# The order of two head pairs in RWKV's and HGRN2's steps, and an issue order between their products

## Chip, core and metric

The kernel runs on one core of one Trainium2 chip, as one program. The metric is the device time of a run in microseconds. One execution was recorded by the hardware profiler; the times of the others are without a profile.

## What is computed

One inference step of a decoder trunk with two layers, for 256 prompt tokens and 8 sequences of 8 new tokens (320 columns in all, width 1024, fp32). A layer is a SwiGLU block, a mixer and a second SwiGLU block. The mixer has three groups of heads beside each other: HGRN2 (4 heads of 64), RWKV-7 (4 heads of 64) and latent attention (8 heads, with a paged cache of 2048 positions for the samples):

```python
for l in range(DEPTH):
    x = x + 0.5 * swiglu(rms_norm(x, W['norm_ffn1'][l]), W['ffn1_wi'][l], W['ffn1_wo'][l])
    p = rms_norm(x, W['norm_mix'][l]) @ W['w_in'][l]
    p_hg, p_rw, p_mla = jnp.split(p, [HG_COLS, HG_COLS + RW_COLS], axis=-1)
    o_hg, hg_s = hgrn2_mixer(p_hg, lbs[l], W['hg_norm'][l], hg_s0[l])
    o_rw, rw_s, rw_sh = rwkv7_mixer(p_rw, rw_sh0[l], rw_s0[l], l, W)
    q_nope, q_pe, c, k_pe = mla_project(p_mla, pos, l, W)
    o_mla = attend(l, q_nope, q_pe, c, k_pe)
    x = x + jnp.concatenate([o_hg, o_rw, o_mla], axis=-1) @ W['w_out'][l]
    x = x + 0.5 * swiglu(rms_norm(x, W['norm_ffn2'][l]), W['ffn2_wi'][l], W['ffn2_wo'][l])
```

RWKV-7 and HGRN2 are recurrences over the tokens. The kernel computes them in blocks of 64 tokens (the samples are a fifth block).

## The kernel before

Activations lie transposed, 128 channels by 320 columns. Dense products take each weight as a rounded part and a remainder in fp32r, three matmuls a tile, and write the PSUM banks `pd`, in the SwiGLU blocks `pr` and `pa` too. Each raw weight block is split by ScalarE (`w<-raw`, L434) and VectorE (L435).

In the mixer several Python generators are woven together by `weave`. In the first part these are the RWKV recurrence (`rw`, then `rw_out`), the rest of the input projection (`rin`, `hg_in`, called `fill`) and the samples' attention (`sample`); in the second part HGRN2 (`hg`), the prompt's attention (`prompt`), the samples' attention still, and the output projection (`w_out`). Each generator gives out a piece of work and says how long its results will take. `weave` keeps a running estimate of TensorE's time, lets the recurrences go as soon as they are due, and fills the time between with the others. A planner then orders each engine's queue when the program is built: it goes by priority (the recurrences and the prompt have a higher one) and by its own estimate of when an instruction's inputs and its PSUM bank are ready. What it has ordered, an engine executes in that order.

Four heads are two pairs of heads (`hp` 0 and 1). A pair's two heads lie in partitions 0 to 63 and 64 to 127, so its small products come in twos on a quarter of the array each (64*64). Each fp32 matmul is two records in the trace. Every pair has a generator of its own, and `together` advances both by one step in each round; a round is a *step* below. The steps of a pair in RWKV are: preparation (elementwise), first products and factors, ten steps of five levels that double an inverse (`X` is evacuated by ScalarE at L1145, the others by VectorE at L1165 and L1171, the factors at L1110), then twelve steps of the recurrence over four blocks of 64 tokens: `R` (L1238), `U` (L1246), and state and output (L1256, L1267), with the samples' block spread over the first of them; at last three steps of `rw_out`. HGRN2 has transposes, exponentials, an elementwise step, and seven steps of products.

Both pairs, in RWKV and in HGRN2, take their PSUM banks from one tag, `pr`, which has three:

```python
    BANKS = {"pd": 2, "pr": 3, "pa": 2, "pv": 1}

    def mm(self, out, w, x, start, stop):
        ...
        self.last = self.nc.tensor.matmul(out, w, x, start=start, stop=stop)
```

A level step and its banks, as an example (L1140 to L1171):

```python
            px = self.bank("pr")
            ...
            nc.scalar.copy(X[:, :n], v5(px, n))
            t0 = self.pe
            if lv < 3:
                factors(1, (0, 1, 2, 3) if lv == 1 else (4,))
```

Of the kernel before, what the change touches and what calls it, by code (L numbers as in the profile page):

```python
# [263 lines left out]
class Kern:  # L264
# [279 lines left out]

    def together(self, *gens):

        gens = list(gens)
        while gens:
            r = None
            for g in list(gens):  # L550
                try:
                    r = next(g)
                except StopIteration:
                    gens.remove(g)
            if gens:
                yield r

# [998 lines left out]
```

## Time and profile before

| | |
|---|---|
| median of 3 runs | 1659.08 us (1657.4 to 1660.34) |
| profiled execution | 1657.07 us |
| its span, first to last instruction | 1655.1 us |
| TensorE busy (matmul) | 1615.0 us, 98% |
| VectorE, ScalarE, GpSimd busy | 957.8, 716.0, 83.6 us |
| mean granted clock of TensorE | 0.993 of full speed |

The span lies 2.0 us below the profiled execution's own time. The mixers lie at about 245 to 606 us (layer 0) and 1064 to 1420 us (layer 1); RWKV's steps at 300 to 457 and 1120 to 1266 us, HGRN2's after them.

### The profile page before, as it was taken

To read this page: it belongs to the slowest core of one execution; us is meant where nothing else is said; L and a number is where in the kernel's file an instruction comes from. 1 tells how busy PE (TensorE), PEld (TensorE's weight loads), DVE (VectorE), ACT (ScalarE), POOL (GpSimd) and SP (SyncE) were. 2 spreads that over 40 slices of the span, in tenths; PEclk is the share of its full clock that TensorE was granted. 3 is DMA by queue.
4 is the path that set the end of the run, shared out by engine and by line. 5 is a ranking of instruction groups with operands and counts; after the bars stand their busy time and mean duration, and the time that the engine had idled before them with its cause. 6 is when DMAs were issued, how large, how long until landed. Compare 5 with 4: busy or idle time off the path is not lost.

```text
span 1655.1 us, 33369 instructions
## 1 busy us (share of the span) xinstructions
PE 1615.0 (98%) x13138; PEld 1441.2 (87%) x13138; DVE 957.8 (58%) x1593; ACT 716.0 (43%) x1207; POOL 83.6 (5%) x118
## 2 busy tenths in 40 slices
PE   8999999999999899999999999999999999999998
PEld 8999998776657599999999999987766676999997
DVE  7555448853445585555465554479444665755543
ACT  6444434543353364444344443346333534544432
POOL 0000000200022000000000000012000310000000
PEclk9999999999999999999999999999999999999999
DMA  8444536646673464445445544365457644454442
GB/s 284 148 149 150 153 90 183 179 134 193 182 219 91 143 215 146 150 153 149 147 149 153 148 147 152 100 187 178 118 173 212 205 134 147 151 149 153 153 146 90
DMA packets 131899, 260.82 MB, mean 158 GB/s; under 512 B 17872, under 2 KB 76816, under 8 KB 131744
## 3 DMA queue, kind: packets, MB, share of 16 engines
q1 hardware_dynamic: 118912, 237.34, 47.5%
q10 hardware_dynamic: 12800, 21.30, 4.3%
q8 instruction: 103, 1.69, 0.4%
q0 software_dynamic: 32, 0.07, 0.1%
q14 instruction: 52, 0.43, 0.1%
HBM read 253.52 MB, written 4.47 MB: 156 GB/s over the span
## 4 chain that ended last, share of the span: by engine, by line
PE 88%; DVE 5%; ACT 3%; DMA 2%; issue 1%; SPq 1%; ACTq 0%; DVEq 0%
PE pd L293 33%; PE pr L293 31%; PE pa L293 18%; PE pv L293 4%; DVE w L435 1%; PE pa L297 1%; ACT S L924 1%; DMA cn<-in_cn 1%; DMA raw<-in_wm 1%; DMA ct<-in_ct 1%; DMA xT<-in_x 0%; DVE kS L458 0%; ACT w L434 0%; DVE rt L1073 0%; ACT L924 0%
## 5 line engine op out<-in xcount | busy, mean ns | idle before, releaser
L435 DVE TENSOR_TENSOR w<-raw,w 128x1024 fp32r<-128x1024 f32 (+1 forms) x390 | 412.6, 1060 | 320.1 <-ACT w L434 313.4
L434 ACT CAST w<-raw 128x1024 fp32r<-128x1024 f32 (+1 forms) x390 | 353.2, 910 | 420.5 <-PE pd L293 192.4
L293 PE MATMUL pd<-xh,w 128*128 128x320 f32 x1792 | 423.7, 316 | 8.3 <-ACT w L434 7.1
L293 PEld LDWEIGHTS pd<-xh,w 128*128 128x128 f32 x1792 | 305.2, 189 | 25.5 <-issue 11.4
L293 PE MATMUL pd<-xl,w 128*128 128x320 f32 x896 | 279.9, 314 | 0.0
L293 PE MATMUL pr<-xh,w 128*128 128x320 f32 x1056 | 240.2, 310 | 0.0
L293 PE MATMUL pa<-xh,w 128*128 128x320 f32 x896 | 201.7, 309 | 0.0
L293 PEld LDWEIGHTS pr<-xh,w 128*128 128x128 f32 x1056 | 178.3, 188 | 0.5
L293 PEld LDWEIGHTS pd<-xl,w 128*128 128x128 f32 x896 | 169.7, 189 | 4.9 <-issue 3.5
L293 PE MATMUL pr<-xl,w 128*128 128x320 f32 x528 | 162.5, 309 | 0.0
L293 PE MATMUL pd<-hh,w 128*128 128x320 f32 x704 | 158.2, 309 | 0.0
L293 PE MATMUL pr<-hh,w 128*128 128x320 f32 x704 | 158.2, 309 | 0.0
L293 PEld LDWEIGHTS pa<-xh,w 128*128 128x128 f32 x896 | 151.0, 188 | 0.0
L293 PE MATMUL pa<-xl,w 128*128 128x320 f32 x448 | 137.6, 309 | 0.0
L293 PE MATMUL pa<-ct,qlat 96*64 96x256 f32 x768 | 122.4, 391 | 2.6 <-ACT qlat L994 1.8
L293 PEld LDWEIGHTS pr<-hh,w 128*128 128x128 f32 x704 | 118.4, 188 | 0.0
L293 PEld LDWEIGHTS pd<-hh,w 128*128 128x128 f32 x704 | 118.4, 188 | 0.0
L293 PE MATMUL pr<-hl,w 128*128 128x320 f32 x352 | 108.8, 309 | 0.0
L293 PE MATMUL pd<-hl,w 128*128 128x320 f32 x352 | 108.8, 309 | 0.0
L482 ACT ACTIVATE fa<-fa 128x320 f32<-128x320 f32 x88 | 41.4, 472 | 134.7 <-DVE fa L481 134.7
L293 PEld LDWEIGHTS pr<-xl,w 128*128 128x128 f32 x528 | 99.1, 188 | 0.3
L293 PEld LDWEIGHTS pa<-ct,qlat 96*64 96x64 f32 x768 | 60.6, 137 | 38.4 <-issue 12.2
(388 smaller groups left out, 1996.6 us busy)
## 6 DMA issues: line engine op xcount, KB each, us to landing
raw<-in_wf SPq DMA_DIRECT2D x264, 512.0 KB, 3.6
ct<-in_ct SPq DMA_DIRECT2D x256, 144.0 KB, 3.0
cn<-in_cn SPq DMA_DIRECT2D x256, 128.0 KB, 2.3
raw<-in_wm ACTq DMA_DIRECT2D x76, 256.0 KB, 3.1
raw<-in_wm SPq DMA_DIRECT2D x50, 256.0 KB, 3.5
xT<-in_x SPq DMA_DIRECT2D x4, 320.0 KB, 6.8
wukt<-in_wukt SPq DMA_DIRECT2D x2, 576.0 KB, 5.5
S<-in_rws SPq DMA_DIRECT2D x4, 256.0 KB, 2.9
```

The costliest lines, as they stand in the source:

```text
L293: self.last = self.nc.tensor.matmul(out, w, x, start=start, stop=stop)
L297: self.nc.tensor.transpose(out, x, ident)
L434: self.cast = nc.scalar.copy(h, src).ins
L435: nc.vector.tensor_tensor(out=lo, in0=src, in1=h.bitcast(F32), op=ALU.subtract)
L482: nc.scalar.activation(a, a, AF.Silu)
L924: nc.scalar.activation(S[p, ch], S[p, ch], AF.Exp, bias=m[:, 5:6], scale=MLA_SCALE, accum_out=m[:, ch:ch + 1])
```

## The change

In each round of `together` the generator that goes second has its TensorE instructions queued behind the last matmul that the first one issued. This is an order of issue, recorded as an edge without a semaphore; instructions of other streams may still stand between. After each round the list is reversed: the pair that went second goes first in the next. Both apply to RWKV (`rw`, `rw_out`) and to HGRN2 (`hg`). Nothing else is changed.

```diff
     def together(self, *gens):
 
+
         gens = list(gens)
         while gens:
-            r = None
+            r, last = None, None
             for g in list(gens):
                 try:
-                    r = next(g)
+                    with self.tc.issue_after(last) if last else ExitStack():
+                        r = next(g)
                 except StopIteration:
                     gens.remove(g)
+                last = self.last.ins
+            gens.reverse()
             if gens:
                 yield r
```

## Rows read from the trace of the kernel before

**Rows 1.** The page: the span and, from part 1, the engines' busy time.

```profile
span 1655.1 us, 33369 instructions
...
PE 1615.0 (98%) x13138; PEld 1441.2 (87%) x13138; DVE 957.8 (58%) x1593; ACT 716.0 (43%) x1207; POOL 83.6 (5%) x118
```

**Rows 2.** Windows, busy us of PE, PEld, DVE, ACT, POOL; clock; DMA share, GB/s.

```profile
300.00:457.00 157.00, 154.71 (x1790) 110.12 (x1789) 87.35 (x169) 66.28 (x138) 15.15 (x21) 0.99 0.59 170
...
1120.00:1266.00 146.00, 140.94 (x1714) 100.79 (x1712) 80.47 (x156) 64.34 (x133) 15.14 (x21) 1.00 0.55 161
```

**Rows 3.** Timeline of TensorE, layer 0's recurrence: start us, us, what, records.

```profile
391.62 0.33 PE L293 MATMUL pr<-R,rwa 64*64 64x64 f32 x4
391.88 1.94 PE L293 MATMUL pa<-ct,qlat 96*64 96x256 f32 x14
393.75 0.66 PE L297 MATMUL pa<-cf,S 128*128 128x128 f32 x4
394.16 0.39 PE L293 MATMUL pd<-xh,w 128*128 128x320 f32 x1
394.48 0.33 PE L293 MATMUL pr<-R,rwa 64*64 64x64 f32 x4
394.74 0.42 PE L293 MATMUL pd<-xl,w 128*128 128x320 f32 x1
```

**Rows 4.** Timeline of TensorE, the same product in a later step.

```profile
433.13 0.45 PE L293 MATMUL pr<-R,rwa 64*64 64x64 f32 x8
433.51 1.51 PE L293 MATMUL pv<-cn,PT 128*64 128x256 f32 x10
```

**Rows 5.** Timeline of TensorE, a short S run and the inside of an F run.

```profile
400.03 0.65 PE L293 MATMUL pv<-cn,PT 128*64 128x256 f32 x4
400.61 0.33 PE L293 MATMUL pr<-Rs,rwa 64*64 64x64 f32 x4
...
441.71 0.46 PE L293 MATMUL pd<-xh,w 128*128 128x320 f32 x2
442.00 0.31 PE L293 MATMUL pd<-xl,w 128*128 128x320 f32 x1
```

**Rows 6.** Timeline: first and last 64*64 run of four stretches (22, 16, 20, 13).

```profile
384.12 1.07 PE L293 MATMUL pr<-S,kkr 64*64 64x512 f32 x4
...
440.91 0.33 PE L293 MATMUL pr<-NK,U 64*64 64x64 f32 x2
...
498.25 0.45 PE L293 MATMUL pr<-hq,hk 64*64 64x64 f32 x8
...
533.05 0.40 PE L293 MATMUL pr<-lf,S 64*64 64x8 f32 x8
...
1198.32 0.33 PE L293 MATMUL pr<-nat,NK 64*64 64x64 f32 x4
...
1251.49 0.33 PE L293 MATMUL pr<-NK,U 64*64 64x64 f32 x2
...
1316.35 0.62 PE L293 MATMUL pr<-hq,hk 64*64 64x64 f32 x14
...
1346.60 0.27 PE L293 MATMUL pr<-AT,EX 64*64 64x64 f32 x1
```

**Rows 7.** Timeline of a wait in layer 0; waits of 1120:1266 (us, times, longest).

```profile
343.25 1.28 ACT L1333 ACT_TABLE_LOAD   x1
...
345.78 0.74 ACT L1145 COPY X<-pr 128x320 f32<-128x320 f32 x2
...
346.25 1.09 PE L293 MATMUL pr<-kkr,bk 64*64 64x128 f32 x16 [2.00 <-ACT X L1145]
...
PE pr L293 <- ACT rwv L1267: 2.1, 1, 2.1
PE pr L293 <- ACT X L1145: 2.0, 1, 2.0
```

**Rows 8.** Groups by line and shape: an evacuation of the recurrence (busy, mean ns).

```profile
L1246 ACT COPY U<-pr 128x64 f32<-128x64 f32 x16 | 3.3, 210 | 22.2 <-PE pr L293 22.2
```

## Prediction

> **What bounds the kernel now.** I read the page first. TensorE is busy 1615.0 of 1655.1 us [rows 1], so I looked at what fills that time rather than at idle time. Next came the windows of the stages that `together` drives. In both layers the RWKV stage keeps TensorE at 154.71 of 157.00 us and 140.94 of 146.00 us, with VectorE and ScalarE near half [rows 2]. The matmul queue sets the length of these stages: time saved in it is time saved, as long as other products are at hand to fill it.
>
> Then I read the timeline of TensorE inside the recurrence, where a pattern shows. Three kinds of product take turns: dense ones on the whole array (128*128, F below), the sample's attention (96*64 and 128*64, S below), and the head pairs' own small ones (64*64 into `pr`, H below). The reader is to see one and the same step of the two pairs at 391.62 and at 394.48 us: R times `rwa`, four records each, with S and F work between them [rows 3]. Forty microseconds on, both pairs' R products stand together as one row of eight at 433.13 [rows 4]. So the planner sometimes joins the pairs and mostly does not.
>
> **What a run costs.** A run here is a stretch of one kind. Start to start, the H run of four takes 391.88 - 391.62 = 0.26 us and the run of eight 433.51 - 433.13 = 0.38 us [rows 3, 4]. Four more records therefore cost 0.12 us, and a run pays 0.26 - 0.12 = 0.14 us for being a run. S: four records take 400.61 - 400.03 = 0.58 us [rows 5], fourteen take 393.75 - 391.88 = 1.87 us [rows 3]. Four records are a pair of products (two sequences side by side), fourteen are three and a half, and a half pair takes as long as a whole one, so (1.87 - 0.58) / 3 = 0.43 us a pair and 0.58 - 0.43 = 0.15 us a run. F: two records take 442.00 - 441.71 = 0.29 us inside a run, 0.145 each; a single one between others takes 394.48 - 394.16 = 0.32 us [rows 3, 5], so about 0.18 us a run. If one H run joins another and its two neighbours of one kind grow together, TensorE saves 0.14 + 0.15 = 0.29 us (S) or 0.14 + 0.18 = 0.32 us (F). I take 0.30 us.
>
> **The change part by part.** Nothing is added to or taken from any engine's work: each matmul, copy and transfer stays, and the number of instructions too. Three things move.
>
> *The tie.* The second pair's matmuls of a step stand behind the last matmul of the first pair's. It orders the queue and is no wait in itself. Without the reversal it would often leave a gap, since the pair that goes second is evacuated second.
>
> *The reversal.* The pair that was last goes first. Its inputs are the last to be ready; the other pair's have then been ready longer, and follow at once. So the joint run starts when the later pair could have started anyway. What is delayed is the pair that was ready earlier. It is off the path: the recurrence of layer 0 runs from 384.12 to 441 us for 12 steps [rows 6], about 4.7 us a step, while an evacuation there takes 210 ns [rows 8]. Work of the other streams covers the delay; if that cover ran out, each step would cost the gap between the pairs, in rows 3 up to 394.48 - 391.62 = 2.9 us, or 24 such steps 69 us. TensorE's busy share in rows 2 speaks against that, and I count nothing.
>
> *Engines and queues behind.* On VectorE and ScalarE the pairs' evacuations swap places in every second step, same work. On SP the loads of the states and the stores of the results swap in the same way between two transfers of equal size; nothing on TensorE waits for the one and not the other. I count nothing for both.
>
> *How many runs join.* In the recurrence I count 22 H runs in layer 0 and 20 in layer 1, for 12 steps each; in HGRN2's products 16 and 13, for 7 steps [rows 6], which hold the first and the last run of each stretch. One run a step would leave 38, so 10 + 8 + 9 + 6 = 33 runs could vanish. The ten steps between (the doubling of the inverse) already have about one run a step, and I expect nothing of them. Not all 33 will join: the pairs share the three `pr` banks. In the recurrence, a step of one pair takes one bank in 5 of 12 steps, two in 5 and three in 2 (read from the code). With one each, both pairs fit; with two or three, the second pair's later product needs a bank that is not yet evacuated, and the planner puts other work before it. The bounds are 0 and 33; I take half, 16, since the steps that fit freely are about that share.
>
> The sum: 16 x 0.30 = 4.8 us less, 9.9 us if all 33 join. The profiled execution took 1657.07 us (span 1655.1 and 2.0 around it) and becomes 1652.3. The median of the runs lies 2.0 us above it, at 1659.08. The forecast for a run is so 1654.3, rounded to 1654.
>
> Two things are left out of the sum and stay in the range. A H run that cuts an S pair in half costs up to 0.43 us more, so runs joined inside S may give more than 0.30. And each layer has one place where TensorE sits still for 2.0 us in a level step: the second pair's factors wait for a bank, whose evacuation (`X`, L1145) stands on ScalarE behind a table load and others' work; layer 1 has another, of 2.1 us, in the recurrence [rows 7]. The order in that level step is already the tied one (X and factors of one pair, then X and factors of the other), so I expect the wait to stay; it may also go, if the step falls elsewhere beside ScalarE's work.
>
> **The rivals.**
>
> *Slower: the tied product waits for its bank.* Tying puts more of one step's products directly behind each other, and with three banks the fourth waits for the first to be evacuated. TensorE's queue is in order, so a wait there holds everything behind it. The place is the ten level steps a layer (two banks a pair) and the seven recurrence steps with two or three. The price of a wait is the 2.0 us of rows 7, and three of 34 such steps pay it now. For: the planner's idea of when ScalarE is done is off by that much in three places. Against: 31 steps do not wait. Three more waits take back 6.0 us, more than the whole 4.8; the fifth makes the kernel slower by more than 0.2%: 1654.3 + 5 x 2.0 = 1664 us.
> The Trainium skill, in "TensorEngine Tiling (Array Packing)", section "PSUM Bottleneck", warns in this direction: tiling speeds TensorE up but not the evacuation of PSUM, which may then be the bottleneck. By that rule the result would be this rival's 1664, by the half-idle VectorE and ScalarE of rows 2 my 1654; rows 7 show that the rule does bite in places.
>
> *No change: the runs don't join.* If banks and in-step evacuations keep the pairs' products apart whatever their order, at most 10 of 33 runs vanish and less than 3.3 us is seen: about 1658 us. For: in HGRN2's first products and in the level steps, evacuations already pace the runs. Against: the recurrence has steps of one tiny product a pair (four records, 0.26 us), and those are the ones seen apart in rows 3.
>
> *More: nearly all join, and waits go.* 33 x 0.30 = 9.9 us, and the two 2.0 us waits of the level steps with them: 13.9 us, 1645 us.
>
> **How the numbers follow.** On this kernel 0.2% of 1659 us, 3.3 us, is about what a measurement tells from no change. Chances: my forecast 0.45 (its own range 1649 to 1656), more 0.10, no change 0.27, slower 0.18. The first two are faster by over 0.2%: 0.55. No change falls within: 0.27. The slower rival gives 0.18. The range takes in the full joining with waits gone at the low end and five new waits at the high end: 1645 to 1664.
>
> **What would show it.** Right: in the profile after, R times `rwa` stands as rows of eight records in nearly all steps of the recurrence; the H runs of the two recurrences fall from 42 to about 32, those of HGRN2 from 29 to about 22; all counts of instructions stay; the RWKV window of each layer is shorter by 1 to 2 us at the same TensorE busy share. Wrong: waits of `pr` matmuls on ScalarE's or VectorE's evacuations over the 6 us of now; a window of the recurrence that is longer with TensorE idle in it, because the delayed pair was on the path after all; or as many H runs as before. If the end of RWKV shifts by more than a few microseconds, HGRN2 and the prompt attention begin later too, and the stage's end would tell what that costs.

## The result and the profile after

The prediction was wrong: 1654.0 us forecast, 1645 to 1664 as its range; the changed kernel takes 1672.05 us (median of 6 runs, 1669.09 to 1675.4) beside 1660.07 us for the kernel before in the same rounds. The ratio is 1.006 with a 95% interval of 1.0043 to 1.0078: 7 to 13 us slower. The profiled execution took 1669.09 us, 12.0 more than the profiled one of before (1657.07), and so stands for the difference of the medians.

The page of the changed kernel, answering to [rows 1]:

```profile
span 1667.1 us, 33347 instructions
...
PE 1609.1 (97%) x13138; PEld 1439.8 (86%) x13138; DVE 954.0 (57%) x1593; ACT 713.9 (43%) x1206; POOL 84.1 (5%) x118
```

The counts of matmuls and VectorE operations stay; one table load of ScalarE is fewer. TensorE is busy 5.9 us *less* than in [rows 1]. Span less busy time gives its idle time: 40.1 us before, 58.0 us after. So 17.9 us of new idle time, less 5.9 us of busy time, make the 12.0 us. The windows of the changed kernel (columns as in [rows 2]):

```profile
300.00:457.00 157.00, 151.25 (x1829) 112.87 (x1828) 82.03 (x165) 63.56 (x133) 14.87 (x21) 0.99 0.60 176
457.00:606.00 149.00, 137.55 (x1238) 97.84 (x1236) 93.62 (x193) 68.08 (x156) 19.40 (x22) 0.95 0.51 155
1120.00:1266.00 146.00, 137.81 (x1605) 102.82 (x1604) 79.95 (x161) 64.01 (x123) 13.38 (x19) 0.99 0.61 179
1266.00:1419.00 153.00, 140.54 (x1389) 95.18 (x1384) 84.38 (x179) 60.45 (x154) 21.16 (x24) 0.96 0.45 140
```

The second and the fourth, HGRN2's half of the mixer, were in the kernel before:

```profile
457.00:606.00 149.00, 141.70 (x1291) 103.07 (x1290) 90.14 (x192) 67.14 (x155) 19.05 (x22) 0.98 0.54 166
1266.00:1419.00 153.00, 147.25 (x1359) 106.51 (x1357) 96.66 (x204) 68.22 (x158) 19.03 (x22) 1.00 0.56 169
```

In all four stretches TensorE idles more than before, and in the two later ones the mean granted clock is lower, 0.95 and 0.96 instead of 0.98 and 1.00. With levels of 1.2 and 2.4 GHz, 0.95 means that a tenth of that stretch ran at the lower one. The Trainium skill says in "Perfetto Trace Analysis", section "Matmul Optimizations", that the matmul engine scales its power with utilization and that matmuls should therefore run back to back. The two later stretches agree; the two earlier ones, with 3.5 and 3.1 us more idle time, are at 0.99 (0.99 and 1.00 before).

What the idle time waited for: the waits view of TensorE in the changed kernel, by stretch (300 to 350, 350 to 457, 457 to 520, 1120 to 1165, 1165 to 1296, 1345 to 1432 us; total us, times, longest):

```profile
PE pa L293 <- DMA ct<-in_ct: 1.7, 1, 1.7
...
PE pa L293 <- DMA ct<-in_ct: 1.7, 3, 1.1
...
PE pr L297 <- ACT rwk L457: 2.1, 1, 2.1
PE pd L293 <- DMA wuk<-in_wuk: 2.1, 1, 2.1
PE pr L293 <- ACT rwk L457: 1.9, 1, 1.9
...
PE pa L293 <- DMA ct<-in_ct: 2.2, 1, 2.2
...
PE pa L293 <- DMA ct<-in_ct: 3.4, 4, 1.1
PE pa L297 <- ACT S L928: 2.8, 1, 2.8
...
PE pd L297 <- DVE wuk L834: 4.0, 1, 4.0
```

With 1.7 us more between 1296 and 1345 us, 10.7 us go to `ct`, tiles of the samples' cache, whose products fill gaps; before it was 0.6 us. The two 2.0 us waits on `X` in the level steps [rows 7] are down to 0.3 and 0.2 us. The two waits on `rwk` stand where RWKV ends and HGRN2 begins (L457 is the activation in RWKV's closing norm that reads a `pr` bank):

```profile
463.81 0.80 PE L293 MATMUL pr<-lo,lora 64*128 64x320 f32 x2 [1.85 <-ACT rwk L457]
...
469.19 0.90 PE L297 MATMUL pr<-cf,lf 128*128 128x128 f32 x3 [2.14 <-ACT rwk L457]
```

Around them the clock is low. The windows from 457 to 475 us, of the changed kernel and then of the kernel before:

```profile
457.00:475.00 18.00, 12.35 (x62) 6.59 (x62) 10.93 (x21) 11.53 (x21) 0.00 (x0) 0.73 0.37 109
457.00:475.00 18.00, 15.11 (x113) 10.62 (x113) 7.78 (x19) 10.29 (x20) 1.63 (x2) 0.97 0.74 217
```

Added up by stage over both layers, TensorE's waits from the first lora product to the last one of `rw_out` are 18.9 us (7.3 before), from there to HGRN2's last product 9.8 us (4.3), and from there to the mixer's end 8.7 us (8.3).

The stages, in us between the starts of first and last products in the timelines (layer 0 / layer 1):

```
                                           before          after
first lora product to first level product  40.4 / 41.1     50.8 / 50.5
level steps, to the last X product         35.5 / 32.7     38.0 / 45.4
to the first R                             14.1 / 11.0     12.7 / 20.8
recurrence, to its last state product      49.4 / 45.2     55.2 / 50.3
to the last product of rw_out              12.7 / 11.2      8.2 / 10.7
RWKV in all                               152.1 / 141.2   165.0 / 177.6
whole mixer from the first lora product   303.7 / 297.1   306.3 / 309.8
```

RWKV is 12.9 and 36.4 us longer, the mixer 2.6 and 12.7 us. The longest new piece that both layers share is the first line. There VectorE shows the lead of one pair over the other. Timeline of VectorE before, layer 0 (the first operation on each pair's lora result, L1071, and each pair's last VectorE operation of the preparation, L1090):

```profile
303.87 0.47 DVE L1071 TENSOR_SCALAR rt<-pr 128x320 f32<-128x320 f32 x1
318.15 0.81 DVE L1090 TENSOR_TENSOR kkr<-kkr,eP 128x640 f32<-128x640 f32 x1
325.30 0.48 DVE L1071 TENSOR_SCALAR rt<-pr 128x320 f32<-128x320 f32 x1
334.24 1.08 DVE L1090 TENSOR_TENSOR kkr<-kkr,eP 128x640 f32<-128x640 f32 x1
```

The same in the changed kernel (L1075, L1094):

```profile
312.90 0.49 DVE L1075 TENSOR_SCALAR rt<-pr 128x320 f32<-128x320 f32 x1 [0.38 <-PE pr L293]
320.71 0.48 DVE L1075 TENSOR_SCALAR rt<-pr 128x320 f32<-128x320 f32 x1
329.14 0.81 DVE L1094 TENSOR_TENSOR kkr<-kkr,eP 128x640 f32<-128x640 f32 x1
334.88 0.81 DVE L1094 TENSOR_TENSOR kkr<-kkr,eP 128x640 f32<-128x640 f32 x1
```

Before, the early pair (pair 0, whose inputs are projected first) leads by 21.4 us and is prepared at 319.0. Now pair 1 goes first in this step, pair 0's products are tied behind it, the lead is 7.8 us, and the first pair is prepared at 330.0. The first of the first products comes at 337.0 instead of 323.8 us, in layer 1 at 1157.6 instead of 1144.5.

The later pair, however, is prepared as early as before, at 335.7 us for 335.3. What moves is the place of the products in TensorE's queue. Before, the later pair's first products and the first level product:

```profile
337.90 0.80 PE L293 MATMUL pr<-bk,kkr 64*64 64x64 f32 x20
...
342.00 0.80 PE L293 MATMUL pr<-sw,NK 64*64 64x64 f32 x20
```

In the changed kernel, both pairs' first products and the first level product:

```profile
336.99 0.80 PE L293 MATMUL pr<-bk,kkr 64*64 64x64 f32 x20
...
344.09 0.80 PE L293 MATMUL pr<-bk,kkr 64*64 64x64 f32 x20
...
350.02 0.80 PE L293 MATMUL pr<-sw,NK 64*64 64x64 f32 x20
```

In the step of the first products the order is reversed: pair 0, now the later one, goes first, 1.3 us after its preparation, and pair 1 is tied behind it, 14.1 us after its own (the trace does not name the pairs; this follows from the order of the change). In both kernels the level steps start behind both pairs' first products, and so 8.0 us later now. Layer 1 shows the same: the later pair is prepared at 1157.0 for 1156.1 us, the first level product comes at 1171.4 for 1162.7.

The runs did not join as hoped. Timeline of TensorE, R of the changed kernel, layer 0:

```profile
400.76 0.28 PE L293 MATMUL pr<-R,rwa 64*64 64x64 f32 x4
...
405.28 0.33 PE L293 MATMUL pr<-R,rwa 64*64 64x64 f32 x4 [0.63 <-ACT U L1250]
...
421.43 0.45 PE L293 MATMUL pr<-R,rwa 64*64 64x64 f32 x8
...
447.75 0.45 PE L293 MATMUL pr<-R,rwa 64*64 64x64 f32 x8
```

R itself stands together in 6 of 8 places, before in 2 of 8. But all H runs of a stretch, counted between the same events on both sides (bounds a little wider than in [rows 6]), are 20 + 25 in the recurrence for 23 + 21, 21 + 18 in HGRN2 for 16 + 13, and 12 + 14 in the level steps (to the last X product) for 10 + 9. What joined in one step came apart in others.

### The profile page after: what moved, and what is told of

The parts are those of the page before. It is cut to its first block, busy times and chain, and to the rows that moved or that the text cites. A ratio compares the mean times of both kernels' runs of the same rounds, so it can differ in the third digit from the quotient of the medians.

```text
span 1667.1 us, 33347 instructions
## 1 busy us (share of the span) xinstructions
PE 1609.1 (97%) x13138; PEld 1439.8 (86%) x13138; DVE 954.0 (57%) x1593; ACT 713.9 (43%) x1206; POOL 84.1 (5%) x118
## 3 DMA queue, kind: packets, MB, share of 16 engines
q1 hardware_dynamic: 118912, 237.34, 46.1%
## 4 chain that ended last, share of the span: by engine, by line
PE 88%; DMA 3%; DVE 3%; ACT 3%; SPq 1%; issue 1%; ACTq 0%; DVEq 0%; POOL 0%
PE pd L293 34%; PE pr L293 31%; PE pa L293 18%; PE pv L293 4%; DMA ct<-in_ct 2%; PE pa L297 1%; DVE w L435 1%; ACT S L928 1%; SPq L942 0%; SPq L899 0%; DMA wuv<-in_wuv 0%; DMA cn<-in_cn 0%; PE pd L297 0%; DMA xT<-in_x 0%; ACT L928 0%
## 5 line engine op out<-in xcount | busy, mean ns | idle before, releaser
L293 PE MATMUL pa<-ct,qlat 96*64 96x256 f32 x768 | 121.1, 396 | 11.1 <-DMA ct<-in_ct 10.7
```

## The experiments

Each kernel was timed in five rounds beside the kernel before. "Idle" is the span less TensorE's busy time in the profiled execution.

```
kernel                                      us (range)                  ratio [95%]              idle
tie without reversal                        1667.45 (1660.08-1674.93)   1.0027 [1.0012, 1.0043]  47.0
reversal without tie                        1682.43 (1679.51-1685.18)   1.0117 [1.0092, 1.0142]  63.3
change in RWKV alone                        1677.32 (1670.90-1679.62)   1.0093 [1.0074, 1.0113]  61.5
change in HGRN2 alone                       1656.23 (1650.48-1664.57)   0.9958 [0.9941, 0.9976]  36.8
RWKV's preparation swapped alone            1684.97 (1676.13-1687.20)   1.0128 [1.0102, 1.0154]  57.4
RWKV from the level steps on                1676.09 (1670.63-1678.96)   1.0076 [1.0053, 1.0099]  53.7
HGRN2: the first step's tie alone           1663.53 (1661.97-1671.18)   1.0016 [0.9999, 1.0034]  48.9
HGRN2 without that first tie                1676.50 (1674.64-1678.28)   1.0088 [1.0062, 1.0114]  51.2
RWKV from the recurrence on                 1690.51 (1685.15-1691.80)   1.0160 [1.0136, 1.0184]  58.2
HGRN2 changed, RWKV tied only               1656.11 (1650.35-1665.81)   0.9968 [0.9945, 0.9991]  38.9
RWKV, started the other way round           1671.51 (1665.45-1677.05)   1.0040 [1.0022, 1.0058]  50.2
both, RWKV started the other way round      1671.48 (1665.02-1677.12)   1.0051 [1.0032, 1.0069]  51.9
caches loaded once: before                  1639.30 (1638.34-1642.34)   0.9854 [0.9832, 0.9877]  36.2
caches loaded once: whole change            1651.42 (1645.91-1653.71)   0.9927 [0.9906, 0.9948]  43.6
caches loaded once: RWKV from recurrence    1640.48 (1637.09-1646.96)   0.9856 [0.9833, 0.9880]  36.7
caches loaded once: HGRN2 alone             1649.59 (1644.06-1652.27)   0.9910 [0.9888, 0.9931]  43.2
caches loaded once: RWKV alone              1650.58 (1647.83-1653.64)   0.9920 [0.9896, 0.9943]  39.0
caches loaded once: preparation alone       1642.61 (1637.73-1651.38)   0.9886 [0.9855, 0.9918]  35.0
```

### The two halves of the edit, the two places

Without the reversal:

```diff
-            gens.reverse()
```

> The tie stays, the reversal is taken out: pair 0 goes first in every step. Theory 'head start' (the loss comes from the reversal, which puts pair 1 first in RWKV's preparation, whose inputs are projected last, so that the tie holds pair 0 back): RWKV's first small products are back near 322 us in layer 0 (changed kernel: 337) and the time is back within 4 us of the kernel before. Rival 'lockstep' (the tie itself stretches every step, whoever goes first): still 8 us or more slower than before, with the ten level steps and the recurrence as long as in the changed kernel. Rival 'stale tie' (HGRN2's first step ties pair 1's transposes to a product of the samples, because transposes are not noted as the last product): HGRN2's exponents still start some 20 us late in layer 0, and 4 to 8 us of loss stay.

Without the tie:

```diff
-                    with self.tc.issue_after(last) if last else ExitStack():
-                        r = next(g)
+                    r = next(g)
```

> The reversal stays, the tie is taken out. Head start: without the tie pair 0's preparation need not wait for pair 1's, so the time is within 4 us of the kernel before, and the runs of small products are about as many as before (42 in the two recurrences). If the order of priority alone does the harm, it is 8 us or more slower, with first products near 337 us. Lockstep and stale tie: as before, within 4 us.

In RWKV alone (`plain` is `together` of before):

```diff
-hg, ... = [self.together(*[self.hg(hp) for hp in range(2)])], ...
+hg, ... = [self.plain(*[self.hg(hp) for hp in range(2)])], ...
```

> The change in RWKV alone; HGRN2's pairs advance as in the kernel before. Head start: nearly the whole loss stays, 8 us or more over before, and RWKV's window is as long as in the changed kernel. Stale tie: the loss is gone, within 4 us of before. Lockstep: most of it stays, since RWKV has 26 of the 33 steps with products.

In HGRN2 alone:

```diff
-rw = [self.together(*[self.chain(self.rw(hp), self.rw_out(hp)) for hp in range(2)])]
+rw = [self.plain(*[self.chain(self.rw(hp), self.rw_out(hp)) for hp in range(2)])]
```

> The change in HGRN2 alone; RWKV's pairs advance as in the kernel before. Stale tie: HGRN2's exponents start some 20 us later than before in layer 0, and 4 us or more are lost. Head start: within 4 us of before. Lockstep: 2 to 4 us lost.

By the halves, the tie alone costs 2 to 7 us, the reversal alone 15 to 24: the reversal is the expensive half, and the tie takes some of its cost back. By place, RWKV's part loses 12 to 19 us and HGRN2's part *wins* 4 to 10, which none of the three theories had expected. With the reversal alone and with RWKV alone the first products come at 340.2 and 338.0 us in layer 0 as in the whole change; with the tie alone at 326.1. That HGRN2 comes late is no loss by itself: with HGRN2 alone its exponentials' first product comes at 498.3 us instead of 478.8, and the kernel is faster.

### Which step of RWKV, which tie of HGRN2

For these and the following, `together` was given the rounds in which it ties and reverses (round 2 is the preparation, 3 the first products, 4 to 13 the level steps, 14 to 25 the recurrence):

```diff
-    def together(self, *gens):
+    def together(self, gens, tie=(), rev=(), fresh=False):
...
-                    with self.tc.issue_after(last) if last else ExitStack():
+                    with self.tc.issue_after(last) if last and n in tie else ExitStack():
...
-                last = self.last.ins
-            gens.reverse()
+                last = None if fresh and self.last is was else self.last.ins
+            if n in rev:
+                gens.reverse()
```

The preparation alone (pair 1 first in round 2, no tie): RWKV with `rev=(1, 2)`.

> No tie anywhere; the pairs change places in one step alone, RWKV's preparation, where pair 1 goes first; all other steps of RWKV and HGRN2 run as before. Theory 'head start' (pair 1's inputs are projected last, and putting it first takes pair 0's lead): most of the loss of the change in RWKV alone (15 us) is here, 8 to 16 us slower than before, first small products near 337 us in layer 0. Rival 'later steps' (the reversal harms in the level steps and the recurrence, where the pair that was evacuated last is now waited for): within 4 us of before, first products near 323 us or the loss made up later.

The change in RWKV from round 4 on: `tie=range(4, 99), rev=range(4, 99)`.

> Tie and reversal in RWKV from its fourth step on (level steps, recurrence, closing steps); its first three steps and all of HGRN2 as before. Head start: within 4 us of before or up to 5 us faster. Later steps: 8 to 16 us slower than before, with first products near 323 us and the level steps and recurrence longer, as in the changed kernel.

One swapped step loses 17 to 26 us, more than the whole change. But the later steps, with the preparation left as it was (first products at 321.6 us), lose 9 to 16 us too: the level steps take 46.0 and 44.3 us for 35.5 and 32.7. So the swapped step of the preparation is one cause and not the only one; and the parts do not add up to the whole.

In HGRN2 there is an oddity: its first step's transposes do not set `self.last`, so in the whole change pair 1's are tied behind a product of the samples that was traced earlier, and start at 497.2 where the view of before has 462.3. That tie alone is `tie=(1,)` in HGRN2; the rest without it is `tie=range(1, 99), rev=range(1, 99), fresh=True`.

> RWKV as before; in HGRN2 nothing but the tie of its first step, which puts pair 1's transposes behind a product of the samples; no reversal. Theory 'late HGRN2' (the gain of the change in HGRN2 alone, 7 us, comes from this tie: HGRN2 begins some 20 us later, leaving work to fill the end of the mixer, and the prompt begins earlier): 4 to 8 us faster than before. Rival 'joined steps' (the gain comes from pairs tied in the later steps): within 3 us of before.

> RWKV as before; in HGRN2 tie and reversal in every step, but a tie only where the first pair has issued a product in this step, so that the transposes are free. Late HGRN2: the gain is gone, within 3 us of before, and the exponents start near 479 us in layer 0. Joined steps: still 4 to 8 us faster than before.

The stray tie costs nothing that can be told from zero (up to 6 us slower), the rest without it 10 to 19 us; together they win 7. Neither theory fits both runs, and again the parts are no sum.

### The recurrence alone, and RWKV the other way round

RWKV with `tie=range(14, 99), rev=range(14, 99)`:

> The tie and the reversal in RWKV from its fourteenth step on only (the sixteen... the recurrence of each pair and what follows it), the preparation, the first products and the level steps in the order of before, HGRN2 as before. If the loss that is left when the preparation keeps its order (12.6 us in the run where the new order begins with the level steps) is made in the level steps, this one is within 3 us of before. If any step in which the pairs change places makes the mixer's chains longer, about 12 steps of the 24 are changed and it loses about half of that, 5 to 8 us, with the last state product later than in before (441.0 and 1251.6 us) by 4 us or more.

HGRN2 with the whole change, RWKV with `tie=range(1, 99)` alone:

> HGRN2 with the whole change, RWKV with the tie and without the reversal. If the parts add up, it is the HGRN2 change's gain of 7 us less the 2 to 4 us that the tie alone cost: 1655 to 1658 us, at or a little under before. If instead what counts is how the two recurrences' ends and the last samples stand at the end of the mixer, the gain of the HGRN2 change is not kept: 1662 us or more, with TensorE's waits after the last HGRN2 step back at 8 us or more in the two layers.

RWKV's generators in the order `(1, 0)`, HGRN2 as before, then with the whole change:

> RWKV with the whole change, but its two pairs start the other way round, so that the preparation step has pair 0 first, as before, and each later step the opposite order of the run with the change in RWKV alone (which was 15.5 us slower than before). HGRN2 as before. If the lost head start of the preparation is what costs, the first products come at about 324 and 1145 us again and at least 10 of the 15.5 us come back: 1662 to 1667 us. If the later steps lose by themselves, as the run from the level steps on suggests, it stays 9 to 13 us slower, 1671 to 1675 us, with the first products early and the level steps long (about 45 us for 35.5).

> The whole change in both, RWKV's pairs started the other way round. If the lost head start of the preparation is what makes the whole change slow, this version is as fast as the change in HGRN2 alone, 1655 to 1658 us, faster than before. If the alternation itself costs, it is slower than before by 4 us or more, 1666 to 1672 us.

The recurrence alone is the slowest kernel of all, 23 to 31 us, beyond both expectations, and HGRN2's last product comes within 3 us of its place in the kernel before, counted from the mixer's first lora product, in both layers. All of the loss stands behind it. Its tail, in the timeline of TensorE, layer 0:

```profile
576.82 0.65 PE L293 MATMUL pv<-cn,PT 128*64 128x256 f32 x4 [0.71 <-DMA cn<-in_cn]
...
579.06 1.72 PE L293 MATMUL pv<-cn,PT 128*64 128x256 f32 x8 [1.59 <-DMA cn<-in_cn]
...
582.29 0.65 PE L293 MATMUL pv<-cn,PT 128*64 128x256 f32 x2 [1.51 <-DMA cn<-in_cn]
```

and the loads of that tile there, from 560 to 586 us (nanoseconds min/median/max, first and last start), with their size from the view of transfers:

```profile
L943 SPq DMA_DIRECT2D cn<-in_cn x22: 332/333/1065, 564.2 to 579.2; - x22
...
cn<-in_cn SPq DMA_DIRECT2D x32, 128.0 KB, 2.2
```

A load comes every (579.2 - 564.2) / 21 = 0.71 us. Four records of `cn,PT` use two of them in 0.58 us [rows 5], one every 0.29 us. So the samples' products can run at full speed only as long as other work stands between them; left over for the end, they run at the pace of their loads. How many are left over is in the windows of tile `cn` (busy us and records of TensorE, weight loads, clock, DMA share, GB/s), first of the recurrence alone:

```profile
300.00:540.00 240.00, 28.83 (x176) 13.71 (x176) 0.99 0.55 161
540.00:600.00 60.00, 17.78 (x112) 9.21 (x112) 0.89 0.40 116
```

then of the kernel before:

```profile
300.00:540.00 240.00, 31.04 (x192) 15.35 (x192) 0.99 0.56 165
540.00:600.00 60.00, 14.10 (x96) 6.83 (x96) 0.97 0.56 180
```

and of HGRN2 alone:

```profile
540.00:600.00 60.00, 11.97 (x96) 6.49 (x96) 0.94 0.52 168
```

With `ct` the leftover after 540 us is 136 records for the slowest kernel, 102 for the kernel before and 96 for HGRN2 alone; TensorE's waits from 540 us to the end of that mixer are 10.7, 4.4 and 2.2 us. So a new theory, for these three kernels first: what counts is how many of the samples are left for the end. (In every kernel 32 of the records of `cn` read a weight that uses the same buffers.) The number alone does not settle it: the whole change has 86 records there, fewer than all three, and loses. The preparation alone fits: behind HGRN2's last product it has 142 and 154 records of the samples left (102 and 112 in the kernel before) and 10.7 and 10.4 us of waits. The kernel with HGRN2 changed and RWKV tied only came out as the sum had it, 1 to 9 us faster than before.

The expectation of early first products failed: in the two flipped kernels these came at 335.6 and 338.9 us, though pair 0 is prepared first, at 317.9 us in the first of them. With the tie and the reversal, the pair that is first in one step stands behind the other in the next, so no order of starting lets one pair lead. The first is 4 to 10 us slower than the kernel before, where 9 to 13 was expected if the later steps lose by themselves, and its level steps are long as expected then (46.1 and 43.5 us); the second is 5 to 11 us slower, as expected if the alternation itself costs.

### The samples' caches loaded once

To take the loads away, each layer loads four `ct` and four `cn` tiles and reads them again for all later pages: the samples' products are all there, on the first pages' data.

```diff
+        res = {}
...
+                    if ("ct", hf, si) in res:
+                        cts.append(res["ct", hf, si])
+                        continue
-                    ct = self.s([KR, 2, 3 * PAGE], "ct", 5)
+                    ct = res["ct", hf, si] = self.s([KR, 2, 3 * PAGE], "ct", 5)
```

and the same for `cn`. This also takes the loads off SyncE's queue, from which weights come too, and the planner orders the program anew, so more than the waits for the tiles changes. More than five buffers of each were not tried.

> The kernel before, with the samples' caches loaded once a layer (four ct and four cn tiles, read again for all later pages): the samples' products are all there, on wrong data, and their loads and the waits for them are gone. It is the base line of the next three. TensorE's waits for ct and cn (about 5 us in the two layers) go: 1650 to 1656 us.

> The whole change, with the samples' caches loaded once a layer. If the change loses because the products that fill the gaps meet cache tiles that have not landed, this one is within 3 us of the kernel before with the same caches. If the pairs' own chains are longer and it is they that end late, it stays 7 to 12 us behind that kernel.

> The change in RWKV from the fourteenth step on alone, which lost 26 us, with the samples' caches loaded once a layer. By the cache tiles nearly all of the 26 us goes: within 5 us of the kernel before with the same caches. By the chains it stays 10 us or more behind it.

> The whole change in HGRN2 alone, which won 7 us, with the samples' caches loaded once a layer. If the gain came from samples that were further on when HGRN2 ended, so that their cache tiles had landed, it is within 2 us of the kernel before with the same caches. If it came from products of the two pairs that stand together, the 7 us are still there.

> The whole change in RWKV alone, HGRN2 as before, with the samples' caches loaded once a layer; to be compared with the kernel before with the same caches (1639.3 us). If a later end of RWKV's chain costs by itself (it ends some 13 to 19 us later, and the products that fill the gaps are used up before the last part), it is 8 us or more behind, 1647 to 1653 us. If RWKV's part lost only through cache tiles that had not landed, it is within 3 us of that kernel.

> Only RWKV's preparation step swapped, with the samples' caches loaded once a layer; without that it lost 21 us. There the first products came 14 to 22 us later and RWKV still ended on time in layer 0, with 11 us of waits in each layer after HGRN2. If the swapped step costs through cache tiles, it is within 3 us of the kernel before with the same caches, 1637 to 1643 us. If the lost head start costs by itself, it is 8 us or more behind.

The base line took 1639.3 us, 11 us less than its expectation. Against it (preparation alone and RWKV alone, taken in other rounds, by the ratios to the kernel before; the stretches are 93 to 103 us long, and each count includes the 32 records named above):

```
                       with the loads   caches loaded once   samples' records left for the last 100 us
recurrence alone       +26 us           +1 us                206, 200   (before with the same: 176, 183)
preparation alone      +21 us           +5 us                184, 196
change in HGRN2 alone   -7 us           +10 us               156, 150
change in RWKV alone   +15 us           +11 us               114, 116
whole change           +10 us           +12 us               106, 108
```

The first line settles the recurrence alone: without the loads its loss is gone. The preparation alone loses most of its loss too; the +5 is the distance of two ratios whose half widths (0.0023 and 0.0032) leave it uncertain by some 6 us, so it may be nothing. HGRN2's gain turns into a loss of 10 us, which neither of its expectations had. So the gain needs the loads, and joined products alone do not bring it. With the loads, 14 and 16 records of the samples were left behind HGRN2's last product, for 102 and 112 in the kernel before; that the gain comes from this was not shown, since the whole change has 14 and 22 there and loses.

The whole change and RWKV alone keep their loss. My reading is that there it is the other end of the same stock: too few samples are left. Windows of `cn` in the kernel before with the caches loaded once, the last 100 us of both mixers:

```profile
501.00:595.00 94.00, 14.18 (x128) 7.97 (x128) 1.00 0.28 89
1307.00:1405.00 98.00, 16.45 (x144) 9.44 (x144) 1.00 0.21 67
```

and of the whole change with the same caches:

```profile
498.00:598.00 100.00, 11.14 (x96) 6.06 (x96) 0.97 0.25 83
1310.00:1410.00 100.00, 11.76 (x98) 6.10 (x98) 0.95 0.21 66
```

There are 48 and 39 `ct` records beside these in the first kernel, 10 and 10 in the second. In the second, TensorE then waits for the last streams themselves, mostly the prompt's attention (`kT`, and at L834 its softmax, in a buffer named `wuk`); its timeline, layer 0:

```profile
545.45 1.13 PE L293 MATMUL pd<-kT,qT 96*128 96x256 f32 x4 [1.85 <-DVE xT L617]
...
564.00 1.50 PE L297 MATMUL pd<-cf,wuk 128*128 128x128 f32 x6 [2.68 <-DVE wuk L834]
```

Waits after HGRN2 are 8.0 and 6.1 us there in the two layers, 2.0 and 1.2 in the first kernel, and the granted clock of the stretch is 0.97 and 0.95 instead of 1.00. RWKV, from the first lora product to the last of `rw_out`, takes 170.9 and 172.8 us there and 152.1 and 150.9 in the first kernel; TensorE does not wait in the recurrence, it does more of the samples in the meantime. Of the 12 us between the medians, the two profiled executions show only 5.5 (4.9 between their spans): the one of the first kernel was its slowest run, that of the second among its faster ones. The rest no trace shows.

## Why the prediction was wrong

**The step that failed** is "The reversal": "What is delayed is the pair that was ready earlier. It is off the path ... Work of the other streams covers the delay ... I count nothing." The delayed pair was on the path, because in both kernels the next step stands behind both pairs: in the step of the first products the earlier pair is now held for 14.1 us after its preparation, and the level steps start 8.0 us later. RWKV becomes 12.9 and 36.4 us longer. Work of the other streams did cover much of that, as the step says, since the mixers grow by 2.6 and 12.7 us only. But it did not cover all: of the 17.9 us of new idle time 11.6 lie within RWKV's own steps, where the work that was to fill the gaps met cache tiles that had not landed (9.0 us on `ct`, none before), and 5.5 between RWKV's end and HGRN2's last product. The lower clock there (0.73 for 0.97 from 457 to 475 us) comes on top. What I argued from, the busy share of [rows 2], shows whether cover is used now, not how much is left. The price that I gave for lost cover, 69 us, was far too high for what happened; the zero was as wrong.

That this cover is a fixed stock, used once, is the reading that fits the six kernels with the caches loaded once: those with 106 to 156 records left for the end lose 10 to 12 us, those with 176 to 206 lose 0 to 5. It is argued from them; no run changed the stock by itself.

**The waits that the profile names are not the whole cause.** 10.7 us of waits for `ct` look like the loss. With the loads taken away these waits cannot occur, and the whole change still loses 12 us; in its trace the waits are now behind HGRN2, 14.1 us for 3.2 in the two layers. For the recurrence alone the same experiment took 25 of 26 us away. Waits for cache tiles were not what decided in one kernel, and were the cause in the other.

**The term of the sum**, "how many runs join", fell as well: 16 of 33 expected, while the recurrence has 45 for 44 and HGRN2 39 for 29, so it earned nothing. R joined (6 of 8 places), which was the pattern I had read in [rows 3, 4] and took for the rest. TensorE's busy time did fall, by 5.9 us; nothing here shows from which runs, and the price of 0.30 us a run was not tested by itself.

**The tie** ("an order of the queue and no wait in itself; without the reversal it would often leave a gap") was about right: alone it costs 2 to 7 us, and with the reversal it is cheaper than the reversal alone.

**The rivals.** The slower one had the sign and another mechanism: waits of `pr` products are 6.9 us in the views of the changed kernel and 6.3 before, not 10 more. Of the 6.9, 4.0 are new waits for a bank, at RWKV's closing norm (L457) and not in the level steps or the recurrence, while the two on `X` shrank. The sum hardly moved, so the rule of the Trainium skill in "TensorEngine Tiling (Array Packing)", section "PSUM Bottleneck", by which I gave 1664 us, bites at that place but does not decide here. Closest were two sentences under what would show it wrong: that the delayed pair was on the path after all, with TensorE idle in a longer window, and that a later end of RWKV delays HGRN2 and the prompt. They should have been a rival with a price.

**Still open.** The parts do not add up (+15 and -7 for +10; one step +21 alone), since any change of an edge gives TensorE's queue another order everywhere, in layer 1 also where the code is the same. Why the recurrence alone leaves more samples to the end, why the change in HGRN2 alone wins, and how much of RWKV's length comes from the level steps, was not separated; nor whether five buffers or SyncE's queue set the pace of the loads.

The version to keep is the change in HGRN2 alone: 0.9958 [0.9941, 0.9976] of the kernel before, so it beats both. Why it wins is not shown, and without the samples' loads it loses; a different cache traffic may undo it.

## What to carry to other kernels

When filler work hides a delay, count the filler: look up what is left of it at the end of the stage, and whether it can run at full speed there, before a delay is put down as free. An alternating order holds both pairs to the later one. And when a wait is named in the profile, take its cause away once before believing it: the loss may only move.

## What was not expected of the hardware

The samples' products, alone at the end, ran at the pace of 128 KB loads that came every 0.71 us, 131072 B / 0.71 us = 185 GB/s, while TensorE could use one every 0.29 us. And in the six kernels with the caches loaded once, the granted clock of the last stretch goes with the idle time: 1.00 in both layers for the three with 0.6 to 2.0 us of waits behind HGRN2, 0.93 to 0.97 for the three with 4.9 to 8.0. So a part of what idle time costs can show as busy time: RWKV alone has 2.8 us more idle time than its base line and 8.5 us more busy time (1612.8 for 1604.3), at a mean clock of 0.986 for 0.992. The whole change, at a mean clock of 0.992, has no more busy time than the base line (1601.8).
